# The stages of a transformer kernel handed over inside one kept order, and the mixers' batches moved apart

## The chip, the core and the metric

The kernel runs on one core of a Trainium2 chip. The metric is the device time of one execution in microseconds (us). Before the change, three runs gave 1498.08 to 1498.81 us, median 1498.59 us. Engines are named PE (TensorE, matrix products), DVE (VectorE), ACT (ScalarE), POOL (GpSimd) and SP (SyncE, which issues most transfers).

## What is computed

A sequence of 256 tokens with 1024 channels goes through two layers of a first block and one layer of a second block. Each layer of the first block adds three stages to the residual `x`: half a SwiGLU feed-forward network (FFN, inner width 2816), a set of mixers, and half of another FFN. An RMS norm stands ahead of each stage.

```python
for l in range(2):
    x = x + 0.5 * swiglu(rms_norm(x, norm_ffn1[l]), ffn1_w_gate[l], ffn1_w_up[l], ffn1_w_down[l])
    proj = rms_norm(x, norm_mix[l]) @ w_in[l]
    y_rwkv = rwkv7_mixer(token_shift(proj[..., :D_SHIFT]), ...)       # 6 heads, a recurrence over tokens
    y_attn = attention_mixer(proj[..., D_SHIFT:D_SHIFT + 3*D_ATTN], ...)  # 6 heads, dilated
    y_conv = conv_mixer(proj[..., D_SHIFT + 3*D_ATTN:], ...)          # depthwise, 31 taps, layer norm
    x = x + concat(y_rwkv, y_attn, y_conv) @ w_out[l]
    x = x + 0.5 * swiglu(rms_norm(x, norm_ffn2[l]), ffn2_w_gate[l], ...)
x = second_block(x, ...)     # attention, conv, pool, w_out, layer norm, conv-FFN, layer norm
```

## The kernel before

The residual lies in SBUF as eight tiles `x[:, d]` of 128 channels by 256 tokens. A product in float32 is made of three matmuls of rounded parts (`mm3`, L283 by way of `mm`): `hi` times `xh`, `hi` times `xl`, `lo` times `xh`. A weight piece of 512 KB is fetched by SP into `raw` (3 buffers); ACT makes `hi` (L272) and DVE makes `lo` (L273). In the trace a product into a bank named `at` is a column of the stage's first matrices (gate, up, w_in) or a small auxiliary product; a product into `mm` belongs to the stage's long accumulation (down, w_out).

**The end of a stage.** `ends` writes the last three parts of the accumulation out in such an order that the eight tiles finish one after another (order `KO`). When tile d is finished, `residual` adds it to `x` on DVE (L465), and `Norm.tile(d)` makes the next stage's operands: `xh` on ACT (L373), `xl` on DVE (L374), the square `sq` on ACT (L380), and the sum of squares on POOL (L383, five adds). The last three sums go through PE: six matmuls `at<-ones,sq`, each counted by the profile as two.

**The start of a stage.** `Norm.end` makes the factor of the norm: `nv` (ACT, L310), a power `ny` (POOL, L305), two transposes that spread it over the partitions (`at<-pk,ny`, L294), and `R` (ACT, L395). The products of the stage do not need R, since it multiplies their results (`gu`, L455, for the FFN; `raws`, L603, for the mixers). In the program they are written behind `Norm.end` all the same. In the FFN, the chain from a result to the next operand is `gu` (DVE), `s` (ACT, L457), `h` (DVE, L459), `hh` (ACT, L442), `hl` (DVE, L444).

**The order on the engines.** A scheduler lists the instructions from the program's order and its own estimates. Where `pinned[0]` is true, the matmuls keep the order in which they are written. Before, this holds only from a point in the mixers (L677) to their end. Each engine works through its own list in order.

**The mixers.** Products of w_in (columns) and of w_out (parts) are taken in small portions from a list of jobs; `run(n)` writes n more of them between the steps of the recurrence, so that PE has work while DVE and ACT make the next operands. On DVE lie the lo pieces, 60 taps of the convolution per layer (`ca`, L635), the masks and the forward substitution (L760 to L763), the softmax of attention (L490, L497) and more. Three small matrices go through a spread on PE and back to DVE: `kk` (L724), and `ka` and `q` (L806, the head norms of attention's k and q). Later come `BK` (L921), the chunk states `S0` (`S`, L1011), the statistics `cs` of the convolution (L1026), and the terms `Dc` (L1001, L1002). The 31 taps of each half of the convolution are written in three bundles.

## Time and profile before

| | |
|---|---|
| median of three runs | 1498.59 us |
| profiled execution, its own time | 1499.71 us |
| its span on the core | 1497.9 us |
| PE busy | 1401.9 us, 94 % |
| DVE busy | 939.2 us, 63 % |
| ACT busy | 776.3 us, 52 % |
| POOL busy | 62.7 us, 4 % |
| mean granted clock of PE | 0.960 |

The granted clock is a share of full speed: 1.00 is 2.4 GHz, 0.50 is 1.2 GHz. PE counts as busy while it runs slowly, so an idle share of 6 % is not all that is lost. The profiled execution is 1.1 us above the median of the runs, 1.8 us of its time lie outside the span.

### The profile page before, as it was taken

The numbers are of one execution on the slowest core, as the hardware profiler recorded it, in microseconds if no ns is written. First come the engines' busy times: TensorE is split into PE (matmuls) and PEld (weight loads), VectorE is DVE, ScalarE is ACT, GpSimd is POOL, SyncE is SP. The second block draws the span as 40 slices with busy tenths as digits, with TensorE's granted clock in tenths as the row PEclk, the third lists the DMA queues.
The fourth block names the chain that finished last, engine by engine and source line by source line (L and its number), as shares of the span: only waits on it lengthen the run. The fifth ranks groups of instructions, "written<-read, shape, count | busy, mean of one in ns | idle before, by whom it ended". The sixth has DMA issues, their size and how long they took to land.

```text
span 1497.9 us, 28590 instructions
## 1 busy us (share of the span) xinstructions
PE 1401.9 (94%) x11806; PEld 1364.4 (91%) x11806; DVE 939.2 (63%) x1642; ACT 776.3 (52%) x1291; POOL 62.7 (4%) x84
## 2 busy tenths in 40 slices
PE   6999989889899999899998988889999999899997
PEld 5999988878799999899997987789999988899997
DVE  5555565897565556455555688655555657677775
ACT  5444446454454445344445546344444567767775
POOL 1000010100100000000002100010000000000000
PEclk9999989989799999899998989889999999999998
DMA  7555543332455555455554333235555554366561
GB/s 236 190 172 189 189 141 113 118 112 65 127 178 188 173 188 174 143 171 189 189 172 138 103 120 96 78 98 184 179 190 180 174 182 126 116 183 182 184 194 59
DMA packets 67570, 231.65 MB, mean 155 GB/s; under 512 B 7624, under 2 KB 11376, under 8 KB 67440
## 3 DMA queue, kind: packets, MB, share of 16 engines
q1 hardware_dynamic: 67440, 229.83, 49.6%
q8 instruction: 92, 1.51, 0.4%
q14 instruction: 38, 0.31, 0.1%
HBM read 227.69 MB, written 2.11 MB: 153 GB/s over the span
## 4 chain that ended last, share of the span: by engine, by line
PE 50%; issue 14%; DVE 4%; ACT 3%; POOL 1%; DMA 1%; POOLq 0%; ACTq 0%; DVEq 0%; SPq 0%
PE at L283 28%; PE mm L283 19%; PE at L288 2%; DVE lo L273 1%; PE at L294 1%; POOL ny L305 1%; ACT hi L272 0%; ACT xh L373 0%; POOL sq L383 0%; ACT sq L380 0%; DMA raw<-win 0%; DVE ca L635 0%; DMA raw<-ffn 0%; DMA raw<-wout 0%; ACT raw L267 0%
## 5 line engine op out<-in xcount | busy, mean ns | idle before, releaser
L273 DVE TENSOR_TENSOR lo<-raw,hi 128x1024 fp32r<-128x1024 f32 (+1 forms) x392 | 479.0, 1223 | 410.6 <-PE at L283 322.7
L272 ACT ACTIVATE hi<-raw 128x1024 fp32r<-128x1024 f32 (+1 forms) x392 | 404.6, 1051 | 423.7 <-PE at L283 225.5
L283 PE MATMUL at<-xh,hi 128*128 128x256 f32 x1808 | 518.2, 287 | 1.5 <-ACT xh L1246 1.5
L283 PE MATMUL at<-xh,lo 128*128 128x256 f32 x1808 | 517.5, 286 | 0.4 <-DVE lo L273 0.4
L283 PE MATMUL at<-xl,hi 128*128 128x256 f32 x1808 | 517.5, 286 | 0.0
L283 PEld LDWEIGHTS at<-xh,hi 128*128 128x128 f32 x1808 | 353.3, 196 | 1.8 <-ACT xh L1246 1.8
L283 PEld LDWEIGHTS at<-xh,lo 128*128 128x128 f32 x1808 | 353.0, 195 | 1.2 <-DVE lo L273 0.6
L283 PEld LDWEIGHTS at<-xl,hi 128*128 128x128 f32 x1808 | 353.1, 195 | 0.1
L283 PE MATMUL mm<-hh,hi 128*128 128x256 f32 x880 | 249.0, 284 | 3.4 <-DVE x L465 3.3
L283 PE MATMUL mm<-hl,hi 128*128 128x256 f32 x880 | 248.9, 284 | 0.1
L283 PE MATMUL mm<-hh,lo 128*128 128x256 f32 x880 | 248.6, 283 | 0.0
L283 PEld LDWEIGHTS mm<-hh,hi 128*128 128x128 f32 x880 | 168.5, 192 | 4.8 <-DVE x L465 3.9
L283 PE MATMUL mm<-xh,hi 128*128 128x256 f32 x544 | 162.9, 304 | 7.5 <-ACT xh L408 3.8
L283 PEld LDWEIGHTS mm<-hl,hi 128*128 128x128 f32 x880 | 168.8, 192 | 0.5 <-DVE hl L444 0.3
L283 PEld LDWEIGHTS mm<-hh,lo 128*128 128x128 f32 x880 | 168.8, 192 | 0.0
L283 PE MATMUL mm<-xl,hi 128*128 128x256 f32 x544 | 159.3, 293 | 0.4
L283 PE MATMUL mm<-xh,lo 128*128 128x256 f32 x544 | 157.8, 291 | 0.0
L283 PEld LDWEIGHTS mm<-xh,hi 128*128 128x128 f32 x544 | 108.3, 202 | 12.3 <-ACT xh L408 4.3
L283 PEld LDWEIGHTS mm<-xl,hi 128*128 128x128 f32 x544 | 109.2, 201 | 1.6 <-DVE xl L409 0.6
L283 PEld LDWEIGHTS mm<-xh,lo 128*128 128x128 f32 x544 | 108.6, 200 | 0.5 <-issue 0.5
L442 ACT ACTIVATE hh<-h 128x256 fp32r<-128x256 f32 x110 | 45.9, 417 | 91.0 <-DVE h L459 83.0
L455 DVE TENSOR_TENSOR gu<-at,R 128x512 f32<-128x512 f32 x88 | 60.1, 683 | 8.8 <-PE at L283 8.8
(292 smaller groups left out, 1366.1 us busy)
## 6 DMA issues: line engine op xcount, KB each, us to landing
raw<-ffn SPq DMA_DIRECT2D x330, 512.0 KB, 4.3
raw<-win SPq DMA_DIRECT2D x60, 512.0 KB, 3.7
raw<-wout SPq DMA_DIRECT2D x24, 512.0 KB, 3.6
raw<-win SPq DMA_DIRECT2D x8, 384.0 KB, 3.2
bias<-dbias SPq DMA_DIRECT2D x12, 128.0 KB, 2.1
lpk<-pack SPq DMA_DIRECT2D x2, 625.0 KB, 5.9
x<-x SPq DMA_DIRECT2D x4, 256.0 KB, 4.0
rows<-ebd SPq DMA_DIRECT2D x16, 64.0 KB, 2.2
```

The lines of the kernel that those rows point to most:

```text
L272: act.activation(hi[:, :n], raw[:, :n], AF.Copy)
L273: dve.tensor_sub(lo[:, :n], raw[:, :n], hi[:, :n].bitcast(F32))
L283: placed(pe.matmul(out, lhsT, rhs, start=start, stop=stop, skip_group_check=True))
L288: m = pe.matmul(*c[:3], start=c[3], stop=c[3] if len(c) < 5 else c[4], skip_group_check=True)
L294: placed(pe.transpose(ps, src, ident))
L305: pool.tensor_tensor(y, v, mhalf.to_broadcast([128, n]), op=OP.pow)
L442: act.activation(hh, h, AF.Copy)
L455: dve.tensor_tensor(gu, b, R[:, None, :].to_broadcast([128, 2, T]), op=OP.mult)
```

## The change

Every stage now knows the next one. `ends(parts, finish, nxt)` fetches the first two pieces of the next stage (`prep`), keeps the order of matmuls as written, and from the fourth finished tile on writes six products of the next stage for tile d-3 behind the three of this one (`LAG`). The next stage then multiplies its second pair of pieces; the sum of squares enters after `SUMS` of these steps (4 steps of three matmuls in the FFN, 3 in the mixers), the spread after `FACTOR` (9 or 10). POOL adds all eight squares (seven adds), and PE sums one tile in two matmuls. In the mixers the first two columns are 9 and 3 and the matmuls are pinned from the start; `tha`, `q` and `k`, `BK`, `Rv`, `yc`, `Dc` and the second half of `run`'s portions stand at other places; spreads use two banks at once; and the taps are written as one batch between `S0` and `cs`.

```diff
-TAIL, AHEAD = 3, 5
+TAIL, AHEAD, LAG = 3, 5, 3
+SUMS, FACTOR = 3, 9
...
-            early.append(piece(A["ffn1_0"], 0, 0))
+            early += [piece(A["ffn1_0"], 0, c * 1024) for c in range(2)]
...
-            n = len(self.hl)
-            if 0 < n < ND - 2:
+            if self.hl:
                 (dve if first else pool).tensor_tensor(sq, sq, self.sq, op=OP.add)
-            if n >= ND - 3:
-                for c in range(2):
-                    mm(self.st[:, c:c + 1], sq[:, c * 128:c * 128 + 128], ones[:, 0:1], n == ND - 3 and c == 0, n == ND - 1)
             self.sq = sq
             self.hl[d] = (xh, xl)
+
+        def stats(self):
+            self.st = bank("at")
+            for c in range(2):
+                mm(self.st[:, c:c + 1], self.sq[:, c * 128:c * 128 + 128], ones[:, 0:1], c == 0, True)
...
+    class Parts:
...
+        def tile(self, d):
+            self.hl[d] = split(x[:, d])
...
-    def ends(parts, finish):
+    def ends(parts, finish, nxt=None):
+        nxt and nxt.prep()
+        pinned[0] = nxt is not None
+        go = nxt and nxt.start()
         for i, d in enumerate(KO):
             for e in KO[:AHEAD] if i == 0 else KO[i + AHEAD - 1:i + AHEAD]:
                 for p in parts[:-1]:
                     p(e)
             parts[-1](d)
             finish(d)
+            if nxt and i >= LAG:
+                next(go)
+        for i in range(LAG if nxt else 0):
+            next(go, None)
...
+        def prep(self, first=None):
+            self.first = first or [piece(self.src, 0, c * 1024) for c in range(2)]
...
+        def start(self, ks=KO):
+            self.b = bank("at").rearrange("p (j t) -> p j t", j=2)
+            for k in ks:
+                for j in range(2):
+                    s = slice(k * 128, k * 128 + 128)
+                    mm3(self.b[:, j], self.first[j][0][:, s], self.first[j][1][:, s], *self.nrm.hl[k],
+                        start=(k == ks[0] and j == 0), stop=(k == ks[-1]))
+                if k != ks[-1]:
+                    yield
...
+            if self.first:
+                pinned[0] = True
+                wd0, = load(0, (2,))
+                ws = load(1)
+                b = space()
+                for n, _ in enumerate(columns(b, *ws[:2], self.nrm.hl)):
+                    if n == SUMS:
+                        self.nrm.stats()
+                    if n == FACTOR:
+                        R = self.nrm.end()
+                pinned[0] = False
+                gate = gate_of(R)
+                rest(0, self.b, wd0)
+                rest(1, b, ws[2])
+                i = 2
...
+            self.w = [piece(self.W, 0, self.col[c]) for c in (9, 3)]
...
-        run(8)
+        pinned[0] = True
+        ks = []
+        cols(2, ks.append, "at")
+        run(SUMS)
+        me.nrm.stats()
+        run(FACTOR - SUMS)
+        R = me.nrm.end()
+        rtok = me.nrm.r
+        shift(me.b, [9, 3], [lora, kT[:, 0]])
+        run(16 - FACTOR)
...
-        for n, t in (("k", k_), ("q", q_)):
+
+        def squares(n, t):
...
-        rbk, rbq = qk_factor("k"), qk_factor("q")
+        rbq = qk_factor("q")
+        run(8, step)
+        rbk = qk_factor("k")
+        qk_spread(q_, gq, rbq)
         run(8, step)
         qk_spread(k_, 1.0, rbk)
-        qk_spread(q_, gq, rbq)
-        run(16, step)
+        dve.tensor_tensor(km_[:, :768], km_[:, :768], kT_[:, :768], op=OP.mult)
+        dve.tensor_tensor(c4(Kt_), c4(km_), Ei[:, :, :, 1:129], op=OP.mult)
+        run(8, step)
...
-        taps(0, 0, 10)
...
         U = chunk_u(0)
+        yv(0)
+        mix[5] = at_[2].out(vtok)
+        br[0] = masked(0, Bt, 1, 1, "br")
+        run(2)
+        b = bank("at")[:, :384].rearrange("p (f i) -> p f i", f=3)
+        for f in range(3):
+            fc = slice(f * 128, f * 128 + 128)
+            mm(b[:, f], BK[:, 0, fc], U[:, fc], f == 0)
+            mm(b[:, f], BK[:, 1, fc], Vt[:, 0, fc], False)
+        for hh in range(2):
+            p = slice(hh * 64, hh * 64 + 64)
+            dve.tensor_tensor(S0[p], b[p, :, p], D[p, :, None].to_broadcast([64, 3, 64]), op=OP.mult)
+
+        for j in range(2):
+            taps(j)
+        cs = bank("at")
+        for j in range(2):
+            mm(cs[:, :T], ones, ca[j], j == 0, j == 1)
+        csq = []
+        for j in range(2):
+            dve.scalar_tensor_tensor(ca[j], cs[:, :T], -1.0 / 256, ca[j], op0=OP.mult, op1=OP.add)
+            csq.append(t1("csq"))
+            act.activation(csq[j], ca[j], AF.Square)
+        chunk_y(0, U)
+        yv(1)
+        br[1] = masked(1, Bt, 1, 1, "br")
+        rv = Rv[1].rearrange("p (f j i) -> p f j i", f=3, j=2)
+        b = [bank("at")[:, :192].rearrange("p (f i) -> p f i", f=3) for hh in range(2)]
+        both([(b[h % 2][:, f], AR[p, f, 1, 0], S0[p, f], f == 0) for h, f, p, hc in heads])
+        for hh in range(2):
+            dve.tensor_tensor(rv[:, :, hh], rv[:, :, hh], b[hh], op=OP.add)
+        run(3)
+        b2 = bank("at")
+        for j in range(2):
+            for c in range(2):
+                mm(b2[:, c:c + 1], csq[j][:, c * 128:c * 128 + 128], ones[:, 0:1], j == 0 and c == 0, j == 1)
+        rc = token_rsqrt(b2[:, :2], 2, 1.0 / 256, 1e-5, "nc")
+        U = chunk_u(1)
...
-        cs = bank("at")
-        for j in range(2):
-            mm(cs[:, :T], ones, ca[j], j == 0, j == 1)
...
-        ends([lambda d, i=i: part(ws[i], 5 + i, d) for i in range(3)], lambda d: finish(d, acc[d // 2][:, d % 2]))
+        ends([lambda d, i=i: part(ws[i], 5 + i, d) for i in range(3)], lambda d: finish(d, acc[d // 2][:, d % 2]), nxt)
...
+    stage = FFN(A["ffn1_0"], nrm)
+    stage.prep(early)
+    for _ in stage.start(range(ND)):
+        pass
     for l in range(NL):
-        R = nrm.end()
-        hl = nrm.hl
         nrm = Norm(f"norm_mix{l}")
-        ffn(A[f"ffn1_{l}"], hl, swiglu(R), residual(0.5, nrm), early=early if l == 0 else ())
+        mixer = Mixers(l, nrm)
+        stage.go(swiglu, residual(0.5, nrm), mixer)
         if l == 0:
             nc.sync.dma_start(pk[:, FIRST:], A["pack"][:, FIRST:])
-        R = nrm.end()
-        last = nrm
         nrm = Norm(f"norm_ffn2{l}")
-        mixers(l, last.hl, R, last.r, residual(1.0, nrm))
-        R = nrm.end()
-        hl = nrm.hl
-        nrm = Norm(f"norm_ffn1{l + 1}") if l + 1 < NL else None
-        ffn(A[f"ffn2_{l}"], hl, swiglu(R), residual(0.5, nrm))
-
-
-    hl = [split(x[:, d]) for d in range(ND)]
+        stage = FFN(A[f"ffn2_{l}"], nrm)
+        mixer.go(residual(1.0, nrm), stage)
+        nrm = Norm(f"norm_ffn1{l + 1}") if l + 1 < NL else Parts()
+        nxt = FFN(A[f"ffn1_{l + 1}"], nrm) if l + 1 < NL else Second(nrm)
+        stage.go(swiglu, residual(0.5, nrm), nxt)
+        stage = nxt
+    pinned[0] = False
```

**On PE, at the handover from the first FFN to the mixers.** Before (numbers tell tiles apart; `mm_171`, `mm_172` are the sums of the last tiles, `sq_2428`, `sq_2441` and `sq_2453` sums of squares, `ny_2460` the factor, `xh_2352` the first operand of the mixers):

```order
L283 MATMUL mm_172<-hh_2313,hi_2254 128x256 [waits DVE_49]
L283 MATMUL mm_172<-hl_2315,hi_2254 128x256
L283 MATMUL mm_172<-hh_2313,lo_2255 128x256
L283 MATMUL at_2351<-ones_78,sq_2428 128x1 [waits PE_49,Pool_49]
L283 MATMUL at_2351<-ones_78,sq_2428 128x1
L283 MATMUL at_2351<-ones_78,sq_2441 128x1 [waits Activation_49]
L283 MATMUL at_2351<-ones_78,sq_2441 128x1
L283 MATMUL at_2351<-ones_78,sq_2453 128x1 [waits Activation_49]
L283 MATMUL at_2351<-ones_78,sq_2453 128x1
L294 MATMUL at_2463<-pk_72,ny_2460 128x128 [waits PE_49,Pool_49]
L294 MATMUL at_2463<-pk_72,ny_2460 128x128
L283 MATMUL at_2477<-xh_2352,hi_2480 128x256 [waits PE_49]
```

Behind the last product of the stage stand the six sums, the spread, and only then the first product of the mixers. After, the place at which the first product of the next stage (`at_2420`) comes:

```order
L284 MATMUL mm_213<-hh_2311,hi_2252 128x256
L284 MATMUL mm_213<-hl_2313,hi_2252 128x256
L284 MATMUL mm_213<-hh_2311,lo_2253 128x256
L284 MATMUL at_2420<-xh_2363,hi_2319 128x256 [waits PE_49,Activation_49]
L284 MATMUL at_2420<-xl_2364,hi_2319 128x256 [waits DVE_49]
L284 MATMUL at_2420<-xh_2363,lo_2320 128x256
L284 MATMUL at_2420<-xh_2363,hi_2325 128x256
L284 MATMUL at_2420<-xl_2364,hi_2325 128x256
L284 MATMUL at_2420<-xh_2363,lo_2326 128x256
L284 MATMUL mm_210<-hh_2311,hi_2252 128x256
L284 MATMUL mm_210<-hl_2313,hi_2252 128x256
L284 MATMUL mm_210<-hh_2311,lo_2253 128x256
```

Four such turns of six and three follow one another; then the products of the last four tiles (24), and the second pair of pieces (`at_2522`), among whose products the two sums (`at_2556`) stand:

```order
L284 MATMUL at_2522<-xh_2396,hi_2525 128x256
L284 MATMUL at_2522<-xl_2397,hi_2525 128x256
L284 MATMUL at_2522<-xh_2396,lo_2526 128x256
L284 MATMUL at_2556<-ones_78,sq_2486 128x1 [waits PE_49,Pool_49]
L284 MATMUL at_2556<-ones_78,sq_2486 128x1
L284 MATMUL at_2522<-xh_2413,hi_2525 128x256
L284 MATMUL at_2522<-xl_2414,hi_2525 128x256
L284 MATMUL at_2522<-xh_2413,lo_2526 128x256
L284 MATMUL at_2522<-xh_2431,hi_2525 128x256
```

The sums have moved behind 33 products that do not need them; the spread follows 18 products later.

**On DVE, at the same handover after the change** (`x_74<-mm_...` finishes a tile, `xl_...` is the operand made from it, `lo_...` a weight piece), the last four tiles to finish:

```order
L530 SCALAR_TENSOR_TENSOR x_74<-mm_210,x_74 128x256 [waits PE_49]
L274 TENSOR_TENSOR lo_2532<-raw_2529,hi_2531 128x1024 [waits DMAHW7_49,Activation_49]
L373 SCALAR_TENSOR_TENSOR xl_2414<-x_74,pk_72,xh_2413 128x256 [waits Activation_49]
L373 SCALAR_TENSOR_TENSOR xl_2432<-x_74,pk_72,xh_2431 128x256 [waits Activation_49]
L530 SCALAR_TENSOR_TENSOR x_74<-mm_211,x_74 128x256 [waits PE_49]
L530 SCALAR_TENSOR_TENSOR x_74<-mm_212,x_74 128x256 [waits PE_49]
L530 SCALAR_TENSOR_TENSOR x_74<-mm_213,x_74 128x256 [waits PE_49]
L373 SCALAR_TENSOR_TENSOR xl_2449<-x_74,pk_72,xh_2448 128x256 [waits Activation_49]
L274 TENSOR_TENSOR lo_2538<-raw_2535,hi_2537 128x1024 [waits DMAHW0_49]
L373 SCALAR_TENSOR_TENSOR xl_2466<-x_74,pk_72,xh_2465 128x256 [waits Activation_49]
L373 SCALAR_TENSOR_TENSOR xl_2483<-x_74,pk_72,xh_2482 128x256 [waits Activation_49]
```

Between the first `x` (eight rows above this piece) and the last `xl` stand three lo pieces, one of them above the piece; before, two of them stood there.

**On DVE in the first mixers, at the end of the taps.** `ca<-z,lpk,ca` is a tap, `S_...` the chunk state, `ca<-at,ca` the first instruction behind the statistics `cs`, `br` and `kr` masks. Before:

```order
L635 SCALAR_TENSOR_TENSOR ca<-z,lpk,ca 128x256 [waits DVE_49] x5
L1001 TENSOR_TENSOR Dc<-at,v 128x256 [waits PE_49]
L635 SCALAR_TENSOR_TENSOR ca<-z,lpk,ca 128x256 [waits DVE_49]
L1002 SCALAR_TENSOR_TENSOR Dc<-Dc,lpk,at 128x256 [waits DVE_49]
L635 SCALAR_TENSOR_TENSOR ca<-z,lpk,ca 128x256 [waits DVE_49]
L1001 TENSOR_TENSOR Dc<-at,v 128x256 [waits PE_49] x2
L1002 SCALAR_TENSOR_TENSOR Dc<-Dc,lpk,at 128x256 [waits DVE_49] x2
L1011 TENSOR_TENSOR S_4122<-at,D 64x192 [waits PE_49]
L1011 TENSOR_TENSOR S_4122<-at,D 64x192
L989 TENSOR_TENSOR y<-y,at 128x3x128 [waits PE_49,Activation_49]
L738 TENSOR_TENSOR br<-at,pk 128x3x128 [waits PE_49] x2
L273 TENSOR_TENSOR lo<-raw,hi 128x1024 [waits DMAHW6_49,PE_49]
```

After:

```order
L833 TENSOR_TENSOR br<-at,pk 128x3x128 [waits PE_49] x2
L720 SCALAR_TENSOR_TENSOR ca<-z,lpk,ca 128x256 [waits DVE_49] x3
L1087 TENSOR_TENSOR S_3997<-at,D 64x192 [waits PE_49]
L1087 TENSOR_TENSOR S_3997<-at,D 64x192
L720 SCALAR_TENSOR_TENSOR ca<-z,lpk,ca 128x256 [waits DVE_49] x11
L1096 SCALAR_TENSOR_TENSOR ca<-at,ca 128x256 [waits PE_49]
L1096 SCALAR_TENSOR_TENSOR ca<-at,ca 128x256 [waits Activation_49]
L1073 TENSOR_TENSOR y<-y,at 128x3x128 [waits PE_49]
```

The terms Dc and the second chunk's y, br and Rv have left the stretch ahead of `cs`; eleven taps now stand between S0 and `cs`, with nothing else among them.

## Rows read from the trace of the kernel before

**Rows 1.** Windows by stage: us; PE, PEld, DVE, ACT, POOL busy; PEclk, DMA share, GB/s.

```profile
18.20:210.20 192.00, 192.00 (x1582) 191.74 (x1581) 108.00 (x143) 88.33 (x118) 1.15 (x1) 1.00 0.59 184
...
224.00:394.40 170.40, 152.91 (x1495) 141.94 (x1494) 124.42 (x311) 88.04 (x181) 13.96 (x18) 0.92 0.34 99
...
811.30:981.30 170.00, 152.43 (x1495) 142.01 (x1494) 123.61 (x306) 87.53 (x180) 13.68 (x16) 0.92 0.32 97
...
995.00:1187.00 192.00, 191.85 (x1593) 191.33 (x1591) 108.83 (x147) 88.67 (x119) 0.00 (x0) 1.00 0.56 176
```

**Rows 2.** Windows of the five handovers and their sum, same columns.

```profile
210.20:224.00 13.80, 7.68 (x37) 7.19 (x36) 7.99 (x14) 6.53 (x15) 6.25 (x9) 0.63 0.39 115
...
981.30:995.00 13.70, 7.84 (x37) 7.34 (x37) 8.51 (x14) 6.43 (x15) 4.06 (x5) 0.64 0.37 116
sum 68.30, PE 38.19 PEld 35.69 DVE 42.62 ACT 31.52 POOL 25.86; mean PE 7.64 PEld 7.14 DVE 8.52 ACT 6.30 POOL 5.17
```

**Rows 3.** Timeline of PE in the first handover: start, us, instruction, [idle, releaser].

```profile
211.53 0.39 PE L283 MATMUL mm<-hh,hi 128*128 128x256 f32 x1 [1.09 <-DVE x L465]
...
216.03 2.72 PE L283 MATMUL at<-ones,sq 128*128 128x1 f32 x12 [3.89 <-POOL sq L383]
219.90 0.69 PE L294 MATMUL at<-pk,ny 128*128 128x128 f32 x2 [1.14 <-POOL ny L305]
220.23 0.56 PE L283 MATMUL at<-xh,hi 128*128 128x256 f32 x1
...
224.01 0.30 PE L283 MATMUL at<-xh,lo 128*128 128x256 f32 x1
```

**Rows 4.** Timeline of DVE in the first handover.

```profile
212.39 0.47 DVE L374 SCALAR_TENSOR_TENSOR xl<-x,pk,xh 128x256 fp32r<-128x256 f32 x1
...
213.65 1.74 DVE L273 TENSOR_TENSOR lo<-raw,hi 128x1024 fp32r<-128x1024 f32 x1
```

**Rows 5.** Groups of DVE and POOL, whole program: busy us, mean ns, idle before.

```profile
L273 DVE TENSOR_TENSOR lo<-raw,hi 128x1024 fp32r<-128x1024 f32 (+1 forms) x392 | 479.0, 1223 | 410.6 <-PE at L283 322.7 <-PE mm L283 30.8 <-issue 28.5
...
L374 DVE SCALAR_TENSOR_TENSOR xl<-x,pk,xh 128x256 fp32r<-128x256 f32 x48 | 27.3, 592 | 5.9 <-ACT xh L373 5.8
...
L465 DVE SCALAR_TENSOR_TENSOR x<-mm,x 128x256 f32<-128x256 f32 x48 | 18.2, 415 | 10.4 <-PE mm L283 10.3
...
L383 POOL TENSOR_TENSOR sq<-sq 128x256 f32<-128x256 f32 x25 | 25.9, 1036 | 604.9 <-ACT sq L380 590.1 <-PE mm L283 11.4 <-DVE x L465 2.3
```

**Rows 6.** Timelines of DVE and ACT around the first gate of the second FFN.

```profile
412.21 0.69 DVE L455 TENSOR_TENSOR gu<-at,R 128x512 f32<-128x512 f32 x1 [7.54 <-PE at L283]
...
412.98 1.28 ACT L457 ACT_TABLE_LOAD   x1 [2.42 <-DVE gu L455]
...
415.54 0.40 ACT L442 ACTIVATE hh<-h 128x256 fp32r<-128x256 f32 x1
```

**Rows 7.** What PE waited for in the first mixers: us, times, longest.

```profile
PE at L294 <- DVE ka L806: 4.6, 1, 4.6
PE at L288 <- ACT BK L921: 3.2, 1, 3.2
```

**Rows 8.** Windows inside the first mixers, columns as in Rows 1.

```profile
257.50:360.40 102.90, 91.91 (x1045) 85.41 (x1044) 90.04 (x250) 53.48 (x115) 7.17 (x13) 0.92 0.32 96
356.90:360.80 3.90, 3.90 (x39) 3.47 (x40) 3.24 (x6) 1.06 (x1) 0.00 (x0) 1.00 0.02 4
367.00:394.40 27.40, 23.59 (x147) 21.00 (x143) 13.97 (x32) 11.37 (x24) 3.09 (x2) 0.81 0.40 103
```

**Rows 9.** Groups of DVE in the first mixers, columns as in Rows 5.

```profile
L635 DVE SCALAR_TENSOR_TENSOR ca<-z,lpk,ca 128x256 f32<-128x256 f32 x60 | 28.4, 477 | 2.0 <-ACT ca L633 1.6
...
L1002 DVE SCALAR_TENSOR_TENSOR Dc<-Dc,lpk,at 128x256 f32<-128x256 f32 x3 | 1.3, 474 | 0.0
```

**Rows 10.** Timeline of PE at the start of the program.

```profile
17.69 0.69 PE L294 MATMUL at<-pk,ny 128*128 128x128 f32 x2 [1.19 <-POOL ny L305]
18.03 0.56 PE L283 MATMUL at<-xh,hi 128*128 128x256 f32 x1
```

More of the change, by code (lines that the diff above doesn't have):

```diff
@@ L846, in mixers @@
         dve.transpose(Y32, X32)
-        taps(0, 10, 20)
         run(8)
+        vtok = [va[:, 0], va[:, 1]]
+        mix[3] = at_[0].out(vtok)
+        att_scores(1)
         sysm = [(n, n // 6, n % 6) for n in range(12)]
+        run(8)
         b = bank("at")[:, :192].rearrange("p (n j) -> p n j", n=12)
@@ L942, in mixers @@
             act.activation(Yf[c][64:96, :, 96:128], b[64:96, c * 6:c * 6 + 6], AF.Copy)
-        run(3)
-        at_[2].turns()
-        taps(1, 20, 31)
-        yT_ = u3("y"); yT = v3(yT_)
-        def yv(c):
-            b = bank("at")[:, :384].rearrange("p (f t) -> p f t", f=3)
-            both([(b[p, f], Vt[:, c, hc], kr[c][:, h], f == 0) for h, f, p, hc in heads])
-            act.activation(yT[:, :, c * 128:c * 128 + 128], b, AF.Copy)
-        run(3)
+        rv_of(1)
+        att_scores(2)
+        run(2)
         for c in range(2):
@@ L969, in mixers, with yv @@
             act.activation(Yf[c][0:64, :, 64:128], b[0:64], AF.Copy)
-        br[0] = masked(0, Bt, 1, 1, "br")
-        yv(1)
-        run(3)
+        kr[1] = masked(1, Kt, 1, 3, "kr")
+        dve.tensor_tensor(km_[:, :768], rT_[:, :768], km_[:, :768], op=OP.mult)
+        at_[2].turns()
+        run(2)
+        def yv(c):
+            b = bank("at")[:, :384].rearrange("p (f t) -> p f t", f=3)
+            both([(b[p, f], Vt[:, c, hc], kr[c][:, h], f == 0) for h, f, p, hc in heads])
+            act.activation(yT[:, :, c * 128:c * 128 + 128], b, AF.Copy)
         S0 = r1("S0")[:, :192].rearrange("p (f i) -> p f i", f=3)
@@ L1098, in finish_out, with __init__, prep, start @@
         nc.sync.dma_start(out.rearrange("p (d t) -> p d t", d=ND), x)
+    class Second:
+        def __init__(self, nrm):
+            self.nrm = nrm
+        def prep(self):
+            self.w = [piece(A["win_2"], 0, j * 1024) for j in range(2)]
+        def start(self):
+            self.b = bank("at")
+            for k in KO:
+                for j in range(2):
+                    s = slice(k * 128, k * 128 + 128)
+                    mm3(self.b[:, j * T:j * T + T], self.w[j][0][:, s], self.w[j][1][:, s], *self.nrm.hl[k],
+                        start=(k == KO[0] and j == 0), stop=(k == KO[-1]))
+                if k != KO[-1]:
+                    yield
     nrm = Norm("norm_ffn10")
@@ L1124, in tile_model @@
     for f in range(4):
[L1125 to L1127 removed]
+        if f:
+            b = bank()
+            colsB(b[:, :T], piece(W, 0, (2 * f) * 1024), hl, True)
+            colsB(b[:, T:], piece(W, 0, (2 * f + 1) * 1024), hl, False)
+        else:
+            b = stage.b
         qk[f] = t3("qk")[:, :512].rearrange("p (j t) -> p j t", j=2)
@@ L1277, in conv_gate @@
         return h
-    ffn(A["ffn_2"], hl, conv_gate, ln.tile, centre=True, tail=3)
+    FFN(A["ffn_2"], hl, centre=True).go(conv_gate, ln.tile)
     ln.end(True)
```

369 lines of the change are left out of this document (170 added, 199 removed).

## The prediction

> **What bounds the kernel now.** The first view is the busy time of each engine by stage. In an FFN nothing is left to win: in the 192.0 us of the first one PE is busy all the time at full clock, and so it is at the end of the last FFN of the first block, where the second block begins [rows 1]. Time is lost elsewhere: in the two mixers, where PE is busy 152.9 and 152.4 of some 170 us at a granted clock of 0.92 [rows 1], and in five handovers between stages, 68.3 us together, where PE is busy 38.2 us at clocks of 0.62 to 0.64 [rows 2].
>
> The second view is the timeline of PE in one handover. The last products of the stage end at about 212.1 us, PE stands 3.89 us until POOL has the sum of squares, needs 2.72 us for twelve small sums, stands 1.14 us for the factor, and then issues the first columns at half speed: 18 of them from 220.23 to 224.01, 0.21 us each [rows 3]. At full speed the FFN's 1582 matmuls take 192.0 us, 0.12 us each [rows 1].
>
> The third view is what PE waits for in the mixers. The longest are `ka`, 4.6 us, and `BK`, 3.2 us [rows 7]. Behind the long waits the clock is low: 0.81 in the stretch that follows the convolution's statistics [rows 8].
>
> **The handovers.** What a handover must hold at full speed are the three last products and the 18 columns inside its window, 21 x 0.12 = 2.5 us. The mean window is 68.3 / 5 = 13.66 us [rows 2], so 11.1 us are lost in each. After the change PE has products to do while the norm is made: from the fourth finished tile on six of the next stage for each three of this one, 18 more behind the last tile's six, then the second pair of pieces. The first pair is now asked for before the last parts, and in front of a mixer the 625 KB of its constants with it; in the handovers the transfers moved 115 GB/s against 184 in an FFN [rows 1, 2], so SP's queue takes this at no cost. What remains:
>
> (a) Two sums and two transposes still run. Twelve sums took 2.72 us, 0.23 each, and the two transposes 0.33 from start to the next start [rows 3]: 0.8 us.
>
> (b) The next stage's products wait for `xl`. From the first finished tile to the product that needs the last `xl`, PE has seven steps of nine matmuls and then the products of three tiles, 18 matmuls: 63 x 0.12 + 18 x 0.12 = 9.7 us. DVE must in this time do eight `x` of 0.42 us [rows 5], eight `xl` of 0.47 where nothing disturbs them [rows 4], and the three lo pieces that the order puts among them at 1.22 [rows 5]: 3.4 + 3.8 + 3.7 = 10.9 us. That is 1.2 us late if nothing else slows DVE. But POOL works beside it: in this handover one lo took 1.74 us and not 1.22, 0.5 more, and an `xl` takes 0.59 us in the mean against 0.47 [rows 4, 5], 1.0 more for eight. That is 1.5 us beside five adds, so 2.1 beside seven, and DVE is 3.3 us late. Between 1.2 and 3.3 I take 2.2 us. POOL itself has seven adds of 1.04 us [rows 5] in steps of 1.08, and keeps pace; the sums stand behind 33 products (4.0 us) that do not need them, which covers the last `xh`, square and add.
>
> So 0.8 + 2.2 = 3.0 us of the 11.1 stay, and 8.1 are gained where the next stage is a mixer (two handovers).
>
> (c) Where the next stage is an FFN (three handovers) the second pair of pieces runs out before the first `hh` is ready. From the factor's transposes to `hh` lie `R`, `gu`, `s`, `h` and `hh`; from the start of `gu` at 412.21 to the end of `hh` at 415.94 it took 3.73 us, of which 1.28 are a table load on ACT [rows 6] that comes where a mixer goes ahead. With R ahead of it that is 4.1 us, or 2.9 without the load, and a second `gu` now may stand in front of `h`; against it PE has 18 matmuls, 2.2 us. PE waits 0.7 to 1.9 us and a little for the second `gu`: I take 1.9. These three gain 6.2 us each.
>
> Sum: 2 x 8.1 + 3 x 6.2 = 34.8 us.
>
> **What the skill says of POOL beside DVE.** The lengthened lo is the row to weigh [rows 4, 5]. The Trainium skill, "SBUF — State Buffer", section "Who interferes with whom", says that a DVE instruction with two SBUF inputs and a GpSimd instruction that reads SBUF exclude each other, whoever comes second being blocked for the whole of the other one. A lo piece, and an `xl`, are of that kind. The row agrees that there is a price; whether each of the adds blocks DVE in full is what no row settles, and that case is the third rival below.
>
> **The start.** The first columns begin at 18.03 us, behind the sums and the factor [rows 10], and run at half clock at first. Afterwards they need only the operands and two pieces. Twelve sums of 2.7 us in all (the form of [rows 3]), a wait of 1.2 and the transposes' 0.3 [rows 10] no longer stand ahead: 4.2 us, of which 0.8 come back later as in (a). The weights may be late instead; between 1 and 4 us I take 3.
>
> **The last handover, into the second block.** There the scheduler has long put products between: PE is busy throughout [rows 1]. Nothing is to win; pinning it may cost up to 1 us. I take 0.
>
> **The mixers.** Waits are taken apart, `Dc` goes behind `cs`, and the taps become one batch ahead of `cs`.
>
> The waits that are named (`ka` 4.6, `BK` 3.2 [rows 7]) get other work in front of them, and with them goes part of the low clock. But DVE takes their place. From `Bt` to `cs` the stretch took 102.9 us, with DVE busy 90.0 and PE 91.9 at clock 0.92 [rows 8]. In the new order DVE has between the same two points everything except `Dc`, three instructions of 0.47 us and three of about the same (2.8 us) [rows 9], and what stood at 356.9 to 360.8, 3.2 us [rows 8]: 84 us. All 60 taps (28.4 us [rows 9]) are still in front of `cs`, and `cs` is a pinned matmul: everything of PE stands behind it. 66 columns or parts fewer stand ahead of `cs` (516 against 582, counted in the order); these 66 x 0.12 = 7.9 us have not gone, they come behind `cs`. PE's own work there is then less than DVE's: of 91.9 us busy the low clock made 102.9 x 0.08 = 8.2, so 91.9 - 8.2 - 7.9 = 76 us. So the stretch saves 102.9 - 84 - 7.9 = 11.0 us if DVE never waits. In the trace it was idle for 12.9 us of the stretch. PE and DVE hand results to each other there, so it will wait somewhat: I take 4 us. (At 12.9 the stretch would be worth -2.)
>
> Behind `cs` the last 27.4 us of the mixer had PE idle for 3.8 us and the clock at 0.81, which is worth 27.4 x 0.19 = 5.2 us more [rows 8]: 9 us lost. There the 7.9 us of moved products and `Dc`'s own matmuls now cover the factors of the convolution's and the heads' norms. But eleven taps (11 x 0.48 = 5.2 us) stand between S0 and `cs`, and PE, with only what is written between them, will stand idle there and start the rest at a low clock. I take 4 of the 9.
>
> In front of `Bt` some waits go and others come; nothing is counted. Together 11.0 - 4 + 4 = 11, less 0.5 for a handful of short new waits: 10.5 us for each of the two mixers, with 2 (DVE as idle as before, half of the rest won) and 23 (DVE never waits, all of the rest won and the waits in front) as ends. Both together: 21 us.
>
> **The sum.** 34.8 + 3 + 0 + 21 = 58.8 us, from 1499.7 us of the profiled execution to 1440.9; the median of the runs stood 1.1 us below that execution, so 1440 us.
>
> **The rivals.**
>
> First, the mixers come out free of stalls: the end at 23 us each gives 25 us more, 1415 us. For it speaks that the order takes apart each named wait; against it the eleven taps ahead of `cs`.
>
> Second, the mixers gain nothing: the wait at `cs` and the low clock behind it take what the others gave. That is 21 us less, 1461 us. For it speaks that DVE was idle 12.9 us in a stretch in which it seemed to have work.
>
> Third, POOL blocks DVE in full in the handovers. Seven adds of 1.04 us are 7.3 us, DVE is 10.9 + 7.3 - 9.7 = 8.5 us late, and a handover gains 6.3 us less: 5 x 6.3 = 31 us, 1471 us. The trace speaks against it: an `xl` grew by 0.12 us in the mean and that lo by 0.5, not by 1.04 [rows 4, 5].
>
> Fourth, on the other side: DVE and PE take turns instead of overlapping. The batch of taps and the pinned products each stand in one list, so a wait of one is a wait of the other. In the stretch from `Bt` to `cs` 84 us of DVE and 76 of PE would at worst add to 160 us, 65 more than the 95 (102.9 - 7.9) that the same work took before; both mixers would lose 130 us, and the kernel come to 1499.7 - 37.8 + 130, about 1591 us at the median. It decides where a mixer loses 19 us, half of what the handovers and the start give: at 114 us, with 30 of PE's 76 us no longer beside DVE's. Against it: before, PE and DVE were busy together for at least 91.9 + 90.0 - 102.9 = 79 us [rows 8].
>
> Fifth, the change does not take effect, because the scheduler had already put products between: so it was at the second block. In the other five the rows show the gap itself, and the order shows it filled. I give this 2 in 100.
>
> **How the numbers follow.** The forecast has 0.54; the first rival 0.12, the second 0.17, the third 0.11, the fourth 0.04, the fifth 0.02. The forecast's own spread is about 1430 to 1452. The range goes from near the first rival to near the third: 1417 to 1468 us. About 0.2 % (3 us) is what a measurement of this kernel can tell from no change. All but the fourth and the fifth are faster than that: 0.94, with 0.02 for no change and 0.04 for slower.
>
> **What would show it.** In the handovers there should be no idle time of PE over 2 us and a granted clock of 1.00; `at<-ones,sq` should come as 4 and not 12, and small waits for `xl` should stand in the list of waits, with none for `sq` but at most one. At the three FFN starts a wait for `hh` or `h` of 1 to 2 us. In the mixers the waits for `ka`, `BK` and `xh` should be gone, a wait of 4 to 8 us should stand at the first reader of `ca`, with the clock at 0.50 behind it, and DVE should be busy over 80 % from `Bt` to `cs`. I am wrong if the sums still wait for POOL for microseconds, if the handovers keep a clock below 0.8, or if DVE is idle for over 10 us in the mixers' stretch.

## The result, and the profile after

The changed kernel takes 1434.55 us in the median (1434.13 to 1436.53), beside 1498.34 us for the kernel before on the same chip: a ratio of 0.9577, 95 % interval 0.9560 to 0.9593, 63.8 us faster. Forecast were 1440 us and 58.8 us.

The first line of the profile's page (busy time, share, instructions):

```profile
PE 1368.2 (95%) x11758; PEld 1333.1 (93%) x11758; DVE 957.2 (67%) x1642; ACT 773.3 (54%) x1291; POOL 74.1 (5%) x92
```

The span is 1432.7 us, 65.2 us shorter. PE's idle time fell from 1497.9 - 1401.9 = 96.0 to 1432.7 - 1368.2 = 64.5 us, 31.5 us less, and its busy time by 33.7 us, though it does the same products and only 48 small sums fewer. The group of these sums, before and then after:

```profile
L283 PE MATMUL at<-ones,sq 128*128 128x1 f32 x72 | 16.5, 354 | 31.3 <-POOL sq L383 17.5 <-DVE sq L383 13.8
```

```profile
L284 PE MATMUL at<-ones,sq 128*128 128x1 f32 x24 | 3.0, 230 | 0.0
```

They are 13.5 of the 33.7 us. The other 20 us or so of busy time are products that are the same in number and take less time: the mean granted clock rose from 0.960 to 0.985. So a wait that was taken away here gave back more than its own length, because slow work stood behind it.

What PE waits for in the changed kernel (us in all, times, longest):

```profile
PE at L284 <- ACT ca L721: 14.1, 2, 7.1
PE at L284 <- DVE xl L373: 11.5, 10, 1.6
PE at L284 <- ACT hi L273: 10.3, 1, 10.3
PE at L284 <- DVE X L935: 4.4, 2, 2.2
PE mm L284 <- ACT hh L478: 3.0, 3, 2.1
...
PE at L295 <- ACT rba L885: 1.3, 4, 0.5
```

No wait for `sq` or `ny` is left in the handovers, and `ka` and `BK` are gone [rows 7]. The first line is the statistics of the convolution, 7.05 us in each mixer. The second is the handovers. The third, 10.3 us, is the start, where PE waits for the first weights.

Windows (us; PE, PEld, DVE, ACT and POOL busy; clock, DMA share, GB/s): the first handover, the stretch from `Bt` to the statistics, the rest of that mixer up to its end, the handover from the first mixer to the FFN, and that from the second:

```profile
205.00:219.00 14.00, 11.69 (x91) 10.96 (x91) 12.43 (x17) 9.60 (x19) 8.93 (x9) 1.00 0.44 126
...
248.30:333.50 85.20, 75.03 (x926) 69.19 (x926) 78.75 (x230) 47.70 (x105) 7.33 (x11) 0.96 0.35 108
333.50:364.00 30.50, 29.88 (x254) 27.68 (x255) 18.59 (x44) 13.45 (x28) 3.12 (x3) 0.95 0.31 92
366.00:380.00 14.00, 10.73 (x78) 9.42 (x77) 12.83 (x22) 6.74 (x16) 6.35 (x7) 1.00 0.30 89
...
921.00:935.00 14.00, 11.40 (x88) 10.48 (x87) 13.10 (x18) 9.12 (x18) 6.87 (x7) 1.00 0.36 114
```

A handover of 14 us held 37 matmuls at a clock of 0.63 [rows 2]; it now holds 91 at 1.00, and PE is idle for 2.3 us. DVE is busy there for 12.4 us of 14, so it has little left to give. In the stretch to the statistics DVE is busy 78.75 of 85.2 us, 92 %.

### The profile page after: what moved, and what is told of

It reads as the page before. It is cut to its first block, busy times and chain, and to the rows that moved or that the text cites. A ratio compares the mean times of both kernels' runs of the same rounds, so it can differ in the third digit from the quotient of the medians.

```text
span 1432.7 us, 28509 instructions
## 1 busy us (share of the span) xinstructions
PE 1368.2 (95%) x11758; PEld 1333.1 (93%) x11758; DVE 957.2 (67%) x1642; ACT 773.3 (54%) x1291; POOL 74.1 (5%) x92
## 5 line engine op out<-in xcount | busy, mean ns | idle before, releaser
L273 ACT ACTIVATE hi<-raw 128x1024 fp32r<-128x1024 f32 (+1 forms) x392 | 412.7, 1054 | 379.5 <-PE at L284 250.4
L284 PE MATMUL at<-xl,hi 128*128 128x256 f32 x1840 | 525.3, 286 | 12.4 <-DVE xl L373 11.5
L284 PE MATMUL at<-xh,hi 128*128 128x256 f32 x1840 | 525.1, 286 | 12.4 <-ACT hi L273 10.3
L284 PE MATMUL at<-xh,lo 128*128 128x256 f32 x1840 | 522.8, 284 | 1.8 <-DVE lo L274 1.8
L284 PEld LDWEIGHTS at<-xh,hi 128*128 128x128 f32 x1840 | 355.5, 193 | 13.3 <-ACT hi L273 10.3
L284 PE MATMUL mm<-xh,hi 128*128 128x256 f32 x512 | 151.5, 296 | 0.0
L284 PE MATMUL mm<-xl,hi 128*128 128x256 f32 x512 | 146.5, 286 | 0.0
L284 PE MATMUL mm<-xh,lo 128*128 128x256 f32 x512 | 146.3, 286 | 0.0
L284 PEld LDWEIGHTS mm<-xh,hi 128*128 128x128 f32 x512 | 99.3, 194 | 4.6 <-issue 2.8
L284 PEld LDWEIGHTS mm<-xl,hi 128*128 128x128 f32 x512 | 99.2, 194 | 0.7 <-issue 0.3
L284 PEld LDWEIGHTS mm<-xh,lo 128*128 128x128 f32 x512 | 99.1, 194 | 0.5 <-issue 0.5
```

The source lines that it names most:

```text
L273: act.activation(hi[:, :n], raw[:, :n], AF.Copy)
L284: placed(pe.matmul(out, lhsT, rhs, start=start, stop=stop, skip_group_check=True))
```

## The experiments

Twelve kernels were run beside the change. `no_adds` and `few_taps` leave work out, so their results are other ones; the rest compute the same. Each ratio is to the kernel before as it ran beside that kernel (95 % interval), so where ratio and median disagree by a few us, the ratio is the fairer figure.

| kernel | us | ratio |
|---|---|---|
| the change | 1434.55 | 0.9577 (0.9560 to 0.9593) |
| hand_only | 1468.71 | 0.9792 (0.9777 to 0.9807) |
| mix_only | 1468.30 | 0.9789 (0.9774 to 0.9803) |
| lag5 | 1432.38 | 0.9547 (0.9533 to 0.9562) |
| cs_late | 1430.72 | 0.9534 (0.9518 to 0.9550) |
| no_adds | 1423.19 | 0.9487 (0.9474 to 0.9500) |
| few_taps | 1414.39 | 0.9431 (0.9418 to 0.9444) |
| factor6 | 1434.32 | 0.9564 (0.9551 to 0.9577) |
| best1 | 1426.84 | 0.9514 (0.9501 to 0.9527) |
| unpinned | 1431.49 | 0.9548 (0.9532 to 0.9564) |
| pe_sums | 1428.08 | 0.9524 (0.9510 to 0.9539) |
| best2 | 1422.27 | 0.9487 (0.9473 to 0.9501) |
| dc_back | 1436.17 | 0.9574 (0.9561 to 0.9587) |

**One part alone.** `hand_only` has the new stages and the old body of the mixers, `mix_only` the old stages and the new body.

```diff
# hand_only, against the change (in mixers, from aug on: the body of before)
-        for j in range(2):
-            taps(j)
+        taps(0, 0, 10)
...
# mix_only, against the kernel before
+        cols(2, ns.append, "at")
+        cols(2, ks.append, "at")
+        run(16)
+        shift(ns[0], [9, 3], [lora, kT[:, 0]])
```

> The new handovers with the old body of the mixers (old order of q, k, BK, Dc, three bundles of taps). If the terms of the sum are separate, as the prediction has them, this gains what the handovers and the start were given, 34.8 + 3 = 38 us: 1460 us against 1498. The waits for ka (4.6 us) and BK (3.2 us) are back in each mixer and the wait at the statistics of the convolution (7.1 us) is gone. Rival: the new mixers need the early start of the handovers or the other way round, so that the handovers alone give under 30 us (above 1468), or nearly all of the 64 us (below 1445).

> The old handovers (sums, factor, then the first product) with the new body of the mixers. By the prediction's terms the mixers alone give 21 us: 1477 us; together with the kernel above the gains should add up to the 64 us measured for both. The five gaps of 13 to 14 us with a clock of 0.63 stand as before. Rival: the mixers' batches only pay when they follow a warm start; then under 12 us, above 1486.

The two gain 30.9 and 31.3 us against the 1499.6 us that the kernel before took beside them, 62.2 together: the parts add up, but the shares are not those of the prediction. `hand_only` was expected at 1460 us and took 1468.71, at the edge of what its rival names; `mix_only` was expected at 1477 and took 1468.30. Waits in `hand_only`:

```profile
PE at L284 <- DVE xl L373: 11.2, 10, 1.6
...
PE at L295 <- DVE ka L896: 7.6, 2, 4.6
PE at L289 <- ACT BK L1011: 6.4, 2, 3.2
...
PE at L284 <- ACT aug L754: 3.7, 2, 1.9
```

`ka` and `BK` are back as expected, and the wait at the statistics is gone. The 3.7 us for `aug` stand in neither of the two kernels that were combined; a likely reason is that two columns that covered it are done earlier. So the handovers and the start together are worth somewhat more than 31 us. Waits in `mix_only`:

```profile
PE at L283 <- POOL sq L383: 17.0, 5, 3.9
...
PE at L283 <- ACT ca L635: 14.1, 2, 7.1
```

The mixers bring 15.7 us each in the mean, not 10.5, although the wait at the statistics is there in full.

**Where the mixers' surplus lies.** The first mixer in three windows, columns as above: from the first finished tile of the FFN ahead of it to `Bt`, from there to the second product of the statistics, and from there to the mixer's last finished tile. First the kernel before, then `mix_only`:

```profile
206.88:254.99 48.11, 39.29 (x287) 37.52 (x286) 26.50 (x42) 29.55 (x58) 9.78 (x11) 0.89 0.39 114
254.99:360.46 105.47, 94.48 (x1066) 87.95 (x1066) 92.57 (x252) 53.92 (x115) 7.79 (x13) 0.92 0.32 96
360.46:400.73 40.27, 31.93 (x217) 28.36 (x215) 22.76 (x51) 18.10 (x38) 6.81 (x7) 0.84 0.39 103
```

```profile
207.25:256.88 49.63, 43.78 (x330) 42.60 (x329) 31.12 (x50) 31.60 (x61) 9.69 (x10) 0.90 0.41 121
256.88:346.21 89.33, 78.43 (x945) 73.05 (x944) 81.59 (x232) 48.66 (x107) 8.00 (x12) 0.95 0.36 107
346.21:386.15 39.94, 35.43 (x290) 32.26 (x288) 26.18 (x61) 19.96 (x43) 5.98 (x7) 0.93 0.33 94
```

What a window loses is counted as the prediction counts it: PE's idle time, and the share of the clock that was not granted times the length. Before, that is 14.1, 19.4 and 14.8 us; in `mix_only` 10.8, 15.4 and 7.3. So 3.3 us are won in front of `Bt`, 4.0 in the stretch and 7.5 behind the statistics, each good to some 0.7 us, since the clock has two digits. In the second mixer it is 4.8, 5.7 and 6.8 by the same windows. The prediction had 0, 7 and 4.

Three things moved behind the statistics: `Dc`, portions of columns and parts, and the second chunk's `y`, `br` and `Rv`. `dc_back` puts the first of them back:

```diff
         U = chunk_u(0)
+        Dc_ = u3("Dc"); Dc = v3(Dc_)
+        for f in range(3):
...
```

> The changed kernel with Dc (six matmuls of PE, six instructions of 0.42 to 0.48 us of DVE) put back in front of the chunk state S0, where it stood. The new mixers gained 31 us and not 21; the step I suspect is the stretch behind the statistics of the convolution, of whose 9 lost us I took 4 as won. If Dc's products are what covers the factors there, waits for the spread of the convolution's and heads' norms return behind the statistics (1 to 3 us, with some of the low clock), and DVE's 2.7 us come back ahead of them: 4 to 6 us per mixer, 1443 to 1447 us. Rival: the portions of columns and parts that moved behind the statistics cover them alone; then only DVE's 2.7 us per mixer are seen, less what PE does beside the taps, 1434 to 1439 us.

It measured 1436.17 us, the change's time within the intervals. New among the waits are only 0.7 us for `U` and 0.6 us for an `xh`, and that for `ca` fell to 12.8 us (2 times). The rival's time holds, so `Dc`'s place does little and the surplus is not its doing. Its reason, the portions alone, is not shown: of the matmuls that read a `hi` or a `lo` only 18 more stand in the third window (156 against 138), and the second chunk's work moved there as well. Which of the two does it was not tried.

**The taps.** `cs_late` writes taps and statistics behind the second chunk, with a portion of products and that chunk's `y` around them; `few_taps` leaves out 28 of 30 multiply-adds of each half of the convolution.

```diff
# cs_late
-        for j in range(2):
-            taps(j)
-        cs = bank("at")
...
         rv = Rv[1].rearrange("p (f j i) -> p f j i", f=3, j=2)
...
+        for j in range(2):
+            taps(j)
+        cs = bank("at")
# few_taps
-            for k in range(30):
+            for k in range(2):
```

> The changed kernel, with the taps and the statistics of the convolution written behind the second chunk's masks, states and Dc. The theory is that the 7.1 us wait at the statistics and the 6.8 us at half clock behind it are DVE's eleven remaining taps with nothing for PE beside them: with other work there the wait falls under 2.5 us and each mixer gains 5 to 8 us, 1419 to 1425 us in all. Rival: DVE is the bound of the whole mixer, so the wait only moves to the next thing that DVE makes (the norm of the convolution or yc) and the time is within 4 us of 1434.5.

> The changed kernel with 2 of the 30 multiply-adds of each half of the convolution (56 taps of 0.48 us left out per mixer, the convolution's result is another one). If DVE bounds the stretch from Bt to the statistics, the wait of 7.1 us there, the 6.8 us at half clock behind it and most of the wait for X (2.2 us) go: 10 to 14 us per mixer, 1406 to 1415 us in all. Rival: the eleven taps behind S0 are an accident of the order and DVE otherwise has slack; then only the wait at the statistics goes, 5.2 of its 7.1 us, and the time is about 1421 us, as with 11 taps fewer.

DVE in the changed kernel ahead of the statistics (start, duration, instruction, [idle, releaser]), and PE:

```profile
325.19 0.71 DVE L1087 TENSOR_TENSOR S<-at,D 64x192 f32<-64x192 f32 x2
325.94 5.69 DVE L720 SCALAR_TENSOR_TENSOR ca<-z,lpk,ca 128x256 f32<-128x256 f32 x11
333.49 0.76 DVE L1096 SCALAR_TENSOR_TENSOR ca<-at,ca 128x256 f32<-128x256 f32 x2 [1.85 <-PE at L284]
...
332.23 1.22 PE L284 MATMUL at<-ca,ones 128*128 128x256 f32 x2 [7.05 <-ACT ca L721]
```

The eleven taps of the order take 5.69 us, ACT finishes `ca`, and PE stands for 7.05 us. Behind it PE runs at half clock for a while:

```profile
333.50:336.40 2.90, 2.90 (x26) 2.57 (x28) 1.30 (x3) 0.89 (x3) 0.00 (x0) 0.50 0.00 0
```

The same stretch, from `Bt` to the statistics, in `few_taps`:

```profile
248.30:324.60 76.30, 74.37 (x933) 69.58 (x932) 58.57 (x177) 46.78 (x106) 7.13 (x11) 0.98 0.38 120
```

Without the taps PE is the bound: 76.3 us, against 85.2. The prediction had 76 us for PE and 84 for DVE; DVE thus costs 9 us here in each mixer, and the whole kernel becomes 20.2 us faster by the medians (some 22 by the ratios), at the slow end of the times that were expected. `cs_late` cut the wait for `ca` from 14.1 to 5.2 us, but gained some 6 us in ratio (0.0043) and not 10 to 15, and its median lies just inside the 4 us that the rival names. The wait for `X` grew from 4.4 to 5.8 us, and 2.2 us for an `xh` are new. So moving the wait helps only in part. That DVE's unchanged total is the reason fits with `few_taps`.

**The handovers' DVE.** `lag5` lets the next stage's products follow five finished tiles behind. `no_adds` leaves POOL's seven adds per handover out.

```diff
# lag5
-TAIL, AHEAD, LAG = 3, 5, 3
+TAIL, AHEAD, LAG = 3, 5, 5
# no_adds
-            if self.hl:
-                (dve if first else pool).tensor_tensor(sq, sq, self.sq, op=OP.add)
+            if self.hl and first:
+                dve.tensor_tensor(sq, sq, self.sq, op=OP.add)
```

> The changed kernel, with the next stage's products five finished tiles behind and not three. The prediction has DVE 2.2 us late at the last xl of each handover, and measured are 11.5 us of waits for xl in all. If this is only a matter of the deadline, two more steps of 1.08 us take it away: waits for xl under 3 us, 8 us faster, about 1426 us. Rival: DVE has more work than PE in the handover whatever the deadline, since POOL's adds lengthen its instructions; then the wait moves to the weight pieces of the second pair and the time is within 3 us of 1434.5.

> The changed kernel without POOL's seven adds of squares in the five handovers (only the last tile's squares are summed, so the norm's factor is another one; no other work changes). In the changed kernel an xl beside an add takes 0.96 us, alone 0.48. If POOL beside DVE is what makes the xl late, every xl is back at 0.48, DVE saves about 2 us in each handover, the waits for xl fall from 11.5 us to under 4, and the time falls by 5 to 8 us. Rival: the lo pieces among the xl (1.22 us each) make them late; then the waits for xl stay above 8 us and the time within 3 us of the changed kernel.

`lag5`: the waits for `xl` fell from ten to five and from 11.5 to 7.0 us, one of up to 1.6 us in each handover. The time is lower by 0.0030 in ratio, with intervals that just overlap, so a gain is likely and not certain. The later deadline thus takes away some 4 of the 11.5 us, not 8 as expected; the wait did not move to the weight pieces either (for `lo` 1.2 us, in the change 1.8). In `no_adds` the waits for `xl` are 4.2 us, and the group of `xl` on DVE reads, in the change and then in `no_adds`:

```profile
L373 DVE SCALAR_TENSOR_TENSOR xl<-x,pk,xh 128x256 fp32r<-128x256 f32 x48 | 33.2, 712 | 8.1 <-ACT xh L372 8.1
```

```profile
L373 DVE SCALAR_TENSOR_TENSOR xl<-x,pk,xh 128x256 fp32r<-128x256 f32 x48 | 22.3, 485 | 7.3 <-ACT xh L372 7.1
```

An `xl` takes 0.71 us in the mean beside seven adds, 0.59 beside five [rows 5], and 0.485 without any. 11.4 us are gained by the medians (some 13 by the ratios), more than the 5 to 8 expected. The waits for `xl` are 7.3 us less. PE's idle time as a whole is 7.1 us less (57.4 us) and its busy time 4.4 us less, at a mean clock of 0.987 against 0.985.

`pe_sums` makes use of it: ACT writes the squares rounded, PE sums them in one matmul per tile, and two transposes bring the sums to the tokens' partitions. The spread of the factor stands two steps earlier. `best2` is this with `cs_late`; `best1` is `cs_late` with `lag5` and `factor6`; `factor6` spreads the factor three steps earlier.

```diff
# pe_sums
+                mm(self.sb[:, :T], ones_r, self.sqs[d], d == KO[0], d == KO[-1])
...
-SUMS, FACTOR = 3, 9
+SUMS, FACTOR = 1, 7
# factor6
-SUMS, FACTOR = 3, 9
+SUMS, FACTOR = 3, 6
```

> The changed kernel with the spread of the norm's factor three steps earlier (after 7 of 16 steps of the second pair in the FFN, 6 in the mixers). The sums stay. The theory of the prediction's step (c): at the start of an FFN PE waits for hh because the chain from R is longer than the 18 products behind the spread; nine more products (1.1 us) cover it, so the waits for hh fall from 3.0 to about 1.0 us and 2 to 3 us are gained. Rival: the spread comes too early for POOL's ny, and PE waits for ny instead, up to 1 us in each of five handovers: no gain or up to 4 us slower.

> Three variants together: statistics of the convolution behind the second chunk, next stage's products five tiles behind, the spread three steps earlier. Alone the first two measured 0.9534 and 0.9547 of the kernel before against 0.9577 for the change. If they are separate, their gains add up: 0.9577 - 0.0043 - 0.0030 - 0.0015 = 0.949 of the kernel before, some 1422 us. Rival: LAG and the earlier spread eat into each other, since with five tiles behind there is less time between the last xl and the factor; then 0.952 or more.

> The changed kernel with the squares summed on PE in place of POOL in the five handovers: ACT writes them rounded, one matmul of 256 columns per tile (8 x 0.12 us) and two transposes (0.33 us) take the place of seven adds on POOL and two sums (0.36 us): PE does 0.9 us more per handover, 4.6 us in all. Leaving the adds out gave 11.4 us. If POOL beside DVE is the cause, 11.4 - 4.6 = 7 us remain, some 1428 us, with xl at 0.48 us in the mean. The factor comes two steps earlier, which alone gave 0 to 2 us. Rival: the 11.4 us came from the sums' chain being shorter without the adds (the factor ready earlier), not from the port; then this longer chain (a copy and two transposes more) gives nothing or loses the 4.6 us, 1434 to 1439.

> The kernel before this one together with the statistics of the convolution behind the second chunk (0.9534 against 0.9577 alone, about 6 us). The two touch different stages, so the gains should add up: about 1422 us, 0.949 of the kernel before. Rival: as with the three variants together, which measured 0.9514 where the sum was 0.949, a part is lost, and it is 0.952 or more.

`factor6`: the waits for `hh` fell from 3.0 to 1.5 us (expected were 1.0), but the time is that of the change within the intervals. `best1`: 0.9514, between the 0.949 of the sum and the 0.952 of the rival; a part is lost. `pe_sums`: 1428.08 us, as expected (1428), with `xl` at 0.49 us. Its rival, that `no_adds` gained by a shorter chain of sums, fails: here the chain is longer, and the gain is there. PE now waits 4.3 us for `ny` in four handovers; the longer chain and the earlier spread were not tried apart. `best2`: 1422.27 us, as expected (1422), the fastest kernel here that leaves nothing out, 0.9 % ahead of the change by the ratios. Its first handover, and its waits:

```profile
205.00:219.00 14.00, 13.03 (x105) 12.40 (x104) 9.74 (x16) 9.59 (x20) 1.43 (x4) 1.00 0.66 193
```

```profile
PE at L286 <- ACT ca L746: 5.2, 2, 2.8
PE at L286 <- DVE X L962: 4.7, 2, 2.7
...
PE at L297 <- POOL ny L308: 2.0, 4, 1.0
PE at L286 <- DVE xl L375: 1.7, 4, 0.4
```

**The kept order.** `unpinned` leaves the matmuls of the handovers to the scheduler, in an FFN also those of its second pair of pieces. In the mixers the order stays kept from their start.

```diff
-        pinned[0] = nxt is not None
+        pinned[0] = False
...
-                pinned[0] = True
                 wd0, = load(0, (2,))
```

> The changed kernel with the order of the handovers' matmuls left to the scheduler (the mixers stay pinned), so that the products of the next stage are there to be taken but their order is not kept. The prediction took the gain from having products beside the norm, not from the pinning. Then the time stays within 6 us of 1434.5. Rival: the kept order is what does it; the scheduler bunches the next stage's products behind the last tiles or pulls the small sums forward, POOL's sum is waited for again, and 3 us or more are lost in each handover: 1450 us or more.

1431.49 us: no slower. What these handovers needed was that the next stage's products are written where they can be taken, not that their order is kept.

## Why the prediction was right

The mechanism stood, and so did the total. The single terms did less well, and some of their misses cancel. The profiles tell the stages apart by the times at which a stage's first tile is finished (the first `x` of each group, L465 before and L530 after; us between these times):

| from, to | before | after | gain | forecast |
|---|---|---|---|---|
| start, first FFN | 206.88 | 202.27 | 4.6 | 3 |
| first FFN, first mixer | 183.44 | 161.45 | 22.0 | 8.1 + 10.5 |
| first mixer, second FFN | 202.60 | 199.60 | 3.0 | 6.2 |
| second FFN, third FFN | 201.70 | 194.83 | 6.9 | 6.2 |
| third FFN, second mixer | 182.60 | 160.95 | 21.6 | 8.1 + 10.5 |
| second mixer, fourth FFN | 202.57 | 194.89 | 7.7 | 6.2 |
| fourth FFN, end | 318.14 | 318.74 | -0.6 | 0 |

In `mix_only` the two rows that hold a mixer gain 13.3 and 16.5 us.

*The handovers, 34.8 us.* By these rows the three into an FFN gave 17.6 us, and the two into a mixer what is left beside `mix_only`, 8.7 and 5.2: some 31 together. Step (b) had DVE 2.2 us late; measured are 11.5 / 5 = 2.3 us of waits for `xl`, and in the first handover 2.3 us idle at full clock. `no_adds` shows that both ends of the bound were rightly named: POOL beside DVE makes the larger part of it. Step (a) priced two rows of 0.23 us, where the two sums are four rows; these take 0.5 us in each of six places at the full clock (3.0 us in all), so that its 0.8 us stood by luck. One of the five failed, from the first mixer to the second FFN. There SP and DVE also work on the second block's position bias: DVE turns round rows (`relo`), twice among the `xl` and twice behind them, and SP waits for each turn before it sends `rel` on, with weights behind it in its queue. At the other handover from a mixer SP issues ten pieces of weights in one run from 907.88 us on. DVE, then SP, then the waits:

```profile
369.19 0.73 DVE L598 STREAM_SHUFFLE relo<-rows 128x512 f32<-128x512 f32 x1
...
373.82 0.72 DVE L598 STREAM_SHUFFLE relo<-rows 128x512 f32<-128x512 f32 x1
```

```profile
369.94 0.34 SPq L599 DMA_DIRECT2D rel<-relo  x1
...
379.72 0.91 SPq L263 DMA_DIRECT2D raw<-ffn  x2
383.09 0.33 SPq L599 DMA_DIRECT2D rel<-relo  x1
383.51 8.25 SPq L263 DMA_DIRECT2D raw<-ffn  x4
```

```profile
PE at L284 <- DVE xl L373: 2.7, 2, 1.6
PE mm L284 <- ACT hh L478: 2.1, 1, 2.1
```

Behind the wait for `hh` PE runs at half clock for 3.4 us, which costs some 1.7 us more:

```profile
387.62:391.03 3.41, 3.41 (x15) 3.37 (x16) 3.41 (x5) 2.52 (x4) 0.00 (x0) 0.50 0.44 121
```

Step (c) gave each FFN start 1.9 us of waiting for `hh`, with 18 matmuls between the factor's transposes and the first product that reads it. Here there are 18, and the wait is 2.1 us, a little over the 2 us at which the prediction drew its line for a handover. At the two other FFN starts 30 and 41 stand there, and PE waits 0.5 us and not at all. So what the prediction left out at this handover is the position bias: "SP's queue takes this at no cost" held in the others. That the late weights are why the order has no more columns here is the likely reading, and was not tried without the bias.

*The start, 3 us.* 4.6, outside its bounds of 1 to 4. The first product is issued at 10.34 us, where before it came at 18.03 [rows 10]. The forecast put 4.2 us at most on what stood directly ahead of 18.03; that products also run between the waits for the first `lo` (1.8 us in all) is not in its sum. The eleven variants with this start finish that tile 4.2 to 6.9 us earlier than the kernel before.

*The last handover into the second block, 0.* The list of waits has nothing there: the ten waits for `xl` are those of the five other handovers. The last row of the table, 0.6 us slower, is in the bounds of what was named.

*The mixers, 21 us.* They gave 31 (`mix_only`; 29.8 by the table's rows). The mechanism stood: DVE is the bound from `Bt` to the statistics, eleven taps stand there, the wait is 7.05 us (forecast 4 to 8) and the clock is half behind it. Three terms were mis-sized, by the windows above. In front of `Bt`, where nothing was counted, 3.3 and 4.8 us were won; the kernel before waits there for `kk` and `tha`, `mix_only` for neither:

```profile
PE at L294 <- DVE kk L724: 3.0, 2, 1.5
...
PE at L283 <- ACT tha L691: 2.5, 2, 1.2
```

In the stretch, 7 were forecast and 4.0 and 5.7 were won. Behind the statistics, "I take 4 of the 9" became 7.5 and 6.8.

The length of the stretch came right by luck: 84 us of DVE and 4 of its waiting were forecast. The change took 85.2 us, with 78.75 of DVE and 6.5 of waiting, and `mix_only` 87.3 us with 79.0 and 8.3:

```profile
259.50:346.80 87.30, 76.40 (x926) 70.51 (x924) 78.97 (x229) 47.80 (x105) 7.26 (x11) 0.94 0.35 106
```

Of DVE's 5 us less, 2.7 are two `lo` pieces that no longer lie in the stretch (16, before 18). And the 66 columns or parts (7.9 us) are not all behind `cs`. In the first mixer the stretch holds 60 matmuls fewer that read a `hi` or a `lo`, but 43 of them now stand in front of `Bt` and 18 behind the statistics.

*The rivals.* The second and fourth are answered by `mix_only`, the fifth by the waits. The third had a true mechanism at too high a price: POOL does hold up DVE, but for 11.4 us in five handovers, not 31. In `few_taps` the first rival can be seen: freed of DVE, a mixer gains 10 us more.

## What to carry to other kernels

Products that do not need a norm's factor belong ahead of it: write the next stage's first products among the last of this one, and look then at the engine that makes their operands, since it is late next. In pricing a wait that goes, count the slow work behind it too: here half of the gain was busy time. When work is moved from one side of a wait to the other, ask what it covers at its new place; behind the statistics some 7 us were won in each mixer, where 4 had been taken. And when a term comes out right, look at its parts: the stretch here had two misses that cancelled.
